# Empty bytes between pools and tiles of a four-layer trunk: other distances between the streamed and the held row of a matmul

## The chip, the cores and the metric

The kernel runs on one core of a Trainium2 chip. The metric is the device time of one launch in microseconds (us). The core has five engines that work side by side, each through its own instruction queue: TensorE (PE) multiplies matrices, VectorE (DVE) and ScalarE (ACT) work element by element, GpSimd (POOL) does small work and starts some transfers, and SyncE (SP) starts most transfers. PE reads two operands from the on-chip memory (SBUF): one that it holds (the weights of the array, loaded ahead; "PEld" in the profile) and one that it streams through, row by row of each partition. Tiles lie in SBUF at byte addresses that the tile pools give out one after another, alike in all 128 partitions.

## The reference

A sequence of 512 vectors of 1,024 numbers in fp32 passes four layers. Each adds a mixer and a SwiGLU feed-forward block (FFN) to the sequence:

```python
for layer in range(4):
    h = rmsnorm(x, norm_mix[layer])
    mix = s5(h) | gla(h) | diff_attention(h) | s5(h)       # layers 0, 1, 2, 3
    x = x + mix
    h = rmsnorm(x, norm_ffn[layer])
    g, u = split(h @ w_gate_up[layer])                      # 1024 -> 2 x 2816
    x = x + (silu(g) * u) @ w_down[layer]                   # 2816 -> 1024
return rmsnorm(x, norm_final)
```

S5 is a complex diagonal recurrence with an output projection (1024 to 2048), GLA is gated linear attention with four heads, the third mixer is differential attention with eight pairs of heads.

## The kernel before, in words

**Arithmetic.** Each fp32 operand of a large product is split into a high part (a rounded copy, `fp32r`) and a low part (what the rounding left), and a product is three matmuls: high by high, high by low, low by high (`mm3`, lines 351 to 353). A weight block is brought by a DMA of 512 KB into a staging tile `wst` (L324, three buffers), cast by ACT into the first half of a tile `whl` (L334, "high", five buffers) and completed by DVE (L338, "low").

**Which row is streamed.** Three forms carry nearly all of PE's time. In `gemm_b` (L351 to L353, `acc<-whl,X`) PE streams 512 columns of the weights `whl` and holds 128 columns of the activations X: `hT` (normed input, transposed), `act` (FFN hidden), `zT` (S5 output), `oT` (output of the attention mixers). In `gemm_a` (`any<-hT,whl`) it streams 512 columns of `hT` and holds the weights. In `seven_product` (L566, the gate and up product of the FFNs of layers 1 to 3, seven products where the plain way needs eight) it streams 256 columns of a tile `sides` or `side` and holds the weights. `sides` are the parts named "11" and "12"; they lie in a buffer of the `hT` pool. The parts "1", "2", "3", "4", "22" are tiles `side...` in the FFN's own pool. A product over one block of 256 hidden columns is 24 matmuls in a row.

**Pools.** `const`, `xp`, `hp` (`hT`), `wp` (`wst`, `whl`), `normp` and `small` stay for the whole program, in this order. Each mixer and each FFN opens a pool of its own behind them, and the next stage's pool lies over the same addresses. A tile laid over one of an earlier stage waits for that tile's last reader; the pool library works this out. The `zT` pools lie at the other end of the memory.

**What sets the order around the change.** Instructions are mostly in an order worked out by a scheduler; at the ends of mixers and the starts of FFNs `hand_all()` fixes the order as written. Before an FFN of layers 1 to 3 starts its first two blocks a and b, SP issues in a row (L599, L324): `slot0`, the first `lent`, `slot1`, the second `lent`, `slot2`, two `wst`, `gain`, one `wst`. `slot0` and `slot1` hold part "21" of the weights; `lent` holds part "1", onto which POOL adds a second block by an accumulating DMA (L602). The order written out there begins: `split21a one:a split21b square flush one:b total1 ... two:a two:b split1b ... five:a ...`. "split21a" is the cast and the low part of `slot0`; "one" and "two" stream `sides` (`a<-sides`, `d<-sides`), "two" with the weights of the slots; "five" streams `side1` with the weights of `lent` (`c<-side`).

In `normed` (L446 to L461) ACT squares a row block and sums it into a tile `ms`, DVE adds eps (L437), POOL raises to -1/2 (L439, `rs`), and the block is scaled.

Of the kernel before, what the change touches and what calls it, by code (L numbers as in the profile page):

```python
# [11 lines left out]
F32 = mybir.dt.float32  # L12
# [9 lines left out]
P = 128  # L22
D = 1024
SEQ = 512
NT = SEQ // P
# [35 lines left out]
class Left:  # L61
# [15 lines left out]
    def room(self):  # L77
        self.hT = [self.tr.hp.tile([P, KT, SEQ], F32R, tag="hT", name=f"hT{z}") for z in range(2)]
# [184 lines left out]
class Trunk:  # L263
    def __init__(self, ctx, tc, ins, out):
        self.ctx, self.tc, self.nc = ctx, tc, tc.nc
        self.i = ins
        self.out = out
        self.rot = 0
        nc = self.nc
        ep = lambda name, bufs, **k: ctx.enter_context(tc.tile_pool(name=name, bufs=bufs, **k))  # L270
        self.cp = ep("const", 1)
        self.xp = ep("xp", 1)
        self.hp = ep("hp", 2)
        self.wp = ep("wp", 3)
        self.np_ = ep("normp", 2)
        self.sp = ep("small", 8)
        self.ps = ep("psum", 1, space=PSUM)
        self.dp = ep("dram", 1, space=DRAM)
        self.ident = self.cp.tile([P, P], F32, name="ident")
        make_identity(nc, self.ident)  # L280
        self.two_pi = float(np.nextafter(np.float32(TWO_PI), np.float32(0)))
        self.mhalf = self.cp.tile([P, 8], F32, name="mhalf")
        nc.vector.memset(self.mhalf[:], -0.5)
        self.ones = self.cp.tile([P, P], F32, name="ones")
        nc.gpsimd.memset(self.ones[:], 1.0)
        self.dq = nc.sync
        self.jobs = iter(())
        self.pend = []
        self.guard, self.lazy = None, False

    def hand_all(self):
        E = mybir.EngineType
# [149 lines left out]
    def normed(self, xt, g, out, pool, aside=False):  # L442

        nc = self.nc
        if pool is None:
            junk = self.wp.tile([P, D], F32, tag="wst", name="sq", bufs=3)  # L446
        else:
            junk = pool.tile([P, D], F32, tag="sq", name="sq", bufs=2)
        ms = self.sp.tile([P, 1], F32, tag="ms", name="ms")
        nc.scalar.activation(junk[:], xt, AF.Square, scale=1.0 / 32.0, accum_out=ms[:])  # L450
        r = self.rsqrt(ms[:], 1, 1e-6)
        if out is None:
            h = pool.tile([P, D], F32, tag="h", name="h", bufs=2)
            nc.vector.scalar_tensor_tensor(h[:], xt, r[:], g[:], op0=ALU.mult, op1=ALU.mult)
            return h
        if aside:
            nc.scalar.mul(junk[:], xt, r[:])
            gr = lambda y: y.rearrange("p (g c) -> p g c", c=16)
            nc.gpsimd.tensor_tensor(out, gr(junk[:]), gr(g[:]), op=ALU.mult)
            return  # L460
        nc.vector.scalar_tensor_tensor(  # L461
            out, xt.rearrange("p (g c) -> p g c", c=16), r[:],
            g[:].rearrange("p (g c) -> p g c", c=16), op0=ALU.mult, op1=ALU.mult,
        )
# [40 lines left out]
    def ffn_plain(self, l, left, after=None, aside=None):  # L505

        nc, i = self.nc, self.i
        wgu, wd = i["ffn_w_gate_up"][l], i["ffn_w_down"][l]
        nxt = None
        with self.tc.tile_pool(name=f"ffn{l}", bufs=1, reuse_waits="tile") as fp:  # L510
            self.jobs = aside(fp) if aside else iter(())
            first = True
            j0 = 0
            for nh in (12, 10):
                acts = []
                for jp in range(j0, j0 + nh, 2):
                    hls, banks = [], []
                    for j in (jp, jp + 1):
                        for half in range(2):
                            hls.append(self.wa(wgu, half * FFN_HIDDEN + j * P))  # L520
                            banks.append(self.anybank())
                            if not first:
                                self.gemm_a(left.hT, hls[-1], banks[-1])
                        if not first:
                            acts.append(self.glu(fp, left.R, banks[-2], banks[-1]))
                            next(self.jobs, None)
                    if first:
                        self.gemm_a4(left, hls, banks)
                        for m in range(2):
                            acts.append(self.glu(fp, left.R, banks[2 * m], banks[2 * m + 1]))  # L530
                        first = False
                        next(self.jobs, None)
                stat = lambda k, part, t: acts[k][:, part, t * P : (t + 1) * P]
                if j0 and after is not None:
                    nxt = Left(self, after)
                for d in range(2):
                    tail = 4 if (d == 1 and j0) else 0
                    self.gemm_b(stat, wd, nh, d * 512, self.add_x(d, nxt, left.r), k0=j0, tail=tail)
                j0 += nh
            for _ in self.jobs:  # L540
                pass
        return nxt
# [169 lines left out]
    def ffn(self, l, left, after=None, turn=False, aside=None):  # L712
# [5 lines left out]
        with self.tc.tile_pool(name=f"ffn{l}", bufs=1, reuse_waits="tile") as fp:  # L718

            room = lambda: fp.tile([P, 2, 4, 256], F32, tag="act", name="lent", bufs=4)  # L720
            left.open(fp, ("1", "2", "4", "3", "22") if l < 3 else ("1", "2"))
            if l == 3:
                lent = room()
            slots = [fp.tile([P, 4, 256], F32, name=f"slot{n}") for n in range(SLOTS)]

            if l < 3:
                lent = room()
            self.jobs = aside(fp) if aside else iter(())
            blocks = [self.seven_block(fp, slots, left, wgu, b, turn) for b in range(FFN_HIDDEN // 256)]
            f = blocks[:2]  # L730
# [15 lines left out]
            for step in plan.split():  # L746
                name, _, n = step.partition(":")
# [633 lines left out]
    def s5_first(self, ctx):  # L1381
        nc, i = self.nc, self.i
        xin = self.xp.tile([P, NT, D], F32, tag="x", name="xin")
        zpool = ctx.enter_context(self.tc.tile_pool(name="zT0", bufs=1, side="right"))
        zT = zpool.tile([P, 2, KT, SEQ], F32R, name="zT")
        with self.tc.tile_pool(name="s5_0", bufs=1) as p:
            scr, more = (self.hp.tile([P, 4096], F32, tag="hT", name=f"scr{z}") for z in range(2))
            oms = [more[:, 1024 * z : 1024 * z + 1024].rearrange("p (a b) -> p a b", a=2) for z in range(2)]
# [73 lines left out]
    def s5_second(self, l, ctx, left):  # L1462
        nc = self.nc
        zpool = ctx.enter_context(self.tc.tile_pool(name="zT1", bufs=1, side="right"))
        zT = zpool.tile([P, 2, KT, SEQ], F32R, name="zT")
        with self.tc.tile_pool(name="s5_1", bufs=1) as p:
            room = p.tile([P, 6, 512], F32, name="room2")
            parts = (("in", 0, 2, 2), ("cs", 2, 5, 3), ("out", 5, 8, 2))
            ops = {}

            def get(kk, name):
                if name == "r4":
                    return ops[kk, "cs"][:, 2]
                if name == "map":
                    return ops[kk, "out"][:, 2]
                return ops[kk, name]

            def loads(kk, names):
                for name, a, b, bufs in parts:
                    if name in names:  # L1480
                        o = p.tile([P, b - a, 512], F32, tag=name, name=name, bufs=bufs)
                        nc.sync.dma_start(o[:], self.spill[kk][:, a:b])
                        ops[kk, name] = o

            def steps(kk):
                if kk + 1 < 8:
                    loads(kk + 1, ("in", "cs"))
                if 1 <= kk < 9:
                    loads(kk - 1, ("out",))

            loads(0, ("in", "cs"))
            accs = self.s5_pipe(1, left.hu, zT, False, room, get, steps, left)
        return self.s5_glu(1, zT, accs, self.i["norm_ffn"][l])
# [32 lines left out]
    def gla(self, l, left, after):  # L1526
# [3 lines left out]
        wo = i["gla_w_o"][0]  # L1530
        self.hand(mybir.EngineType.PE)
        with self.tc.tile_pool(name="gla", bufs=1) as p:
            big = lambda name, tag="g8", bufs=5: p.tile([P, 4, 512], F32, tag=tag, name=name, bufs=bufs)
            late = lambda name: big(name, "g8late", 3)
            oT = [p.tile([P, 2, 4, SEQ], F32R, name="oT0"), None]
# [108 lines left out]
            def readout(hf, t):  # L1644
                st, o_h = sts[hf], on[hf]
                oo = row(self.tp("op"))
                ms = self.sp.tile([P, 2], F32, tag="ms2", name="ms")
                for z in range(2):
                    h = 2 * hf + z
                    zs = slice(z * 256, (z + 1) * 256)  # L1650
# [139 lines left out]
    def diff(self, l, left, after):  # L1790
# [2 lines left out]
        w, wo = i["diff_w_qkv"][0], i["diff_w_o"][0]  # L1793
        self.hand(mybir.EngineType.PE)
        with self.tc.tile_pool(name="diff", bufs=1) as p:
            T = lambda tag, bufs=2: p.tile([P, 512], F32, tag=tag, name=tag, bufs=bufs)
            oT = [p.tile([P, 2, 4, SEQ], F32R, name="oT0"), None]
            qks = [p.tile([P, 2, 4, SEQ], F32, tag="qk", name="qk", bufs=2) for _ in range(2)]
# [157 lines left out]

            def normalised(j):
                st, o_s = kept.pop(j)
                q2 = self.sp.tile([P, NT], F32, tag="q2", name="q2")
                v.tensor_tensor(q2[:], st[:, 0], st[:, 0], op=ALU.mult)  # L1960
                v.scalar_tensor_tensor(q2[:], q2[:], 1e-5, st[:, 1], op0=ALU.mult, op1=ALU.add)
                rs = self.rsqrt(q2[:], NT, 0.0)
# [50 lines left out]
            for i in range(32):  # L2013
# [5 lines left out]
                if i in (15, 28, 31):  # L2019
                    n = (0, 0)  # L2020
# [117 lines left out]
```

## Time and profile before

| | us |
|---|---|
| median of 3 runs | 2384.86 (2382.88 to 2385.13) |
| the profiled execution's own time | 2382.31 |
| its span in the profile | 2380.6 |
| PE busy | 2269.0 (95%) |
| DVE busy | 1487.1 (62%) |
| ACT busy | 1073.0 (45%) |
| POOL busy | 266.8 (11%) |

The mean TensorE clock granted over the span is 0.982 of full speed. PE's busy time is not to be read as work at full rate: a matmul's record lasts until its modelled end, and the next one starts while it still runs. What a matmul costs the path is the distance from one start to the next, and that is read from stretches in which PE waits for nothing: from the chain of work, which merges consecutive matmuls of one line and gives their time and count, or from a window of fixed length and the count of matmuls in it.

### The profile page before, as it was taken

The page shows a single profiled execution, that of the slowest core. Times are in us where ns is not written, and L with a number is a line of the kernel's source. Part 1 is how long each engine was busy: PE and PEld are TensorE (multiplying, and loading weights), DVE is VectorE, ACT ScalarE, POOL GpSimd, SP SyncE. Part 2 cuts the span into 40 slices and gives each one's busy share as a digit, 9 for nine tenths or more (in the row PEclk, how much of TensorE's full clock was granted, in tenths as well). Part 3 has the DMA queues.
Part 4 walks back from the last instruction along what each step waited for, and adds up shares of the span by engine and source line. Part 5 has one row for each costly group of instructions (what it writes and reads, how often), then busy time and mean ns, then how long its engine had stood idle before and what let it go on. Part 6 is the DMA issues. An engine that isn't in the chain of part 4 may idle for free. (4 is left out here: it accounts for less than half of the span.)

```text
span 2380.6 us, 35208 instructions
## 1 busy us (share of the span) xinstructions
PE 2269.0 (95%) x14055; PEld 1962.8 (82%) x14055; DVE 1487.1 (62%) x2311; ACT 1073.0 (45%) x1749; POOL 266.8 (11%) x335
## 2 busy tenths in 40 slices
PE   4799999999999999999999998989999899999997
PEld 3578888788877789898987887888989788999996
DVE  7774565555443459585753666875847874967674
ACT  4463445444352346252544665653635233634442
POOL 3330100111000011010001221110000000101000
PEclk9699999999999999999999999999999899999999
DMA  4123344544332258564345465694732645666521
GB/s 110 34 52 138 95 138 143 166 129 166 118 103 85 71 143 208 137 177 124 111 142 117 107 133 145 170 243 115 195 98 89 214 158 150 170 179 154 162 76 67
DMA packets 275502, 317.42 MB, mean 133 GB/s; under 512 B 45653, under 2 KB 214377, under 8 KB 274058
## 3 DMA queue, kind: packets, MB, share of 16 engines
q1 hardware_dynamic: 227210, 238.14, 31.9%
q0 software_dynamic: 48128, 77.02, 15.7%
q8 instruction: 111, 1.82, 0.3%
q14 instruction: 53, 0.43, 0.1%
HBM read 275.92 MB, written 23.99 MB: 126 GB/s over the span
## 5 line engine op out<-in xcount | busy, mean ns | idle before, releaser
L338 DVE TENSOR_TENSOR whl<-wst,whl 128x1024 fp32r<-128x1024 f32 x294 | 359.0, 1223 | 363.1 <-ACT whl L334 362.3
L334 ACT CAST whl<-wst 128x1024 fp32r<-128x1024 f32 x294 | 308.4, 1050 | 530.5 <-PE acc L353 354.8
L566 PE MATMUL a<-side,whl 128*128 128x256 f32 x2376 | 291.2, 279 | 14.2 <-ACT r L638 6.0
L566 PEld LDWEIGHTS a<-side,whl 128*128 128x128 f32 x2376 | 281.4, 190 | 16.2 <-ACT whl L334 6.9
L351 PE MATMUL acc<-whl,act 128*128 128x512 f32 x704 | 276.5, 393 | 0.7 <-DVE g L611 0.7
L353 PE MATMUL acc<-whl,act 128*128 128x512 f32 x704 | 276.9, 393 | 0.0
L352 PE MATMUL acc<-whl,act 128*128 128x512 f32 x704 | 275.6, 391 | 0.0
L566 PE MATMUL c<-side,whl 128*128 128x256 f32 x1584 | 192.4, 278 | 3.6 <-DVE whl L338 3.6
L566 PEld LDWEIGHTS c<-side,whl 128*128 128x128 f32 x1584 | 186.9, 189 | 4.0 <-DVE whl L338 4.0
L351 PEld LDWEIGHTS acc<-whl,act 128*128 128x128 f32 x704 | 132.2, 188 | 30.9 <-DVE g L611 1.9
L352 PEld LDWEIGHTS acc<-whl,act 128*128 128x128 f32 x704 | 132.2, 188 | 28.8
L353 PEld LDWEIGHTS acc<-whl,act 128*128 128x128 f32 x704 | 132.3, 188 | 27.9
L351 PE MATMUL any<-hT,whl 128*128 128x512 f32 x384 | 151.7, 395 | 0.0
L352 PE MATMUL any<-hT,whl 128*128 128x512 f32 x384 | 149.6, 390 | 0.0
L353 PE MATMUL any<-hT,whl 128*128 128x512 f32 x384 | 149.6, 389 | 0.0
L351 PE MATMUL acc<-whl,hT 128*128 128x512 f32 x352 | 143.8, 408 | 1.1 <-ACT whl L334 0.6
L352 PE MATMUL acc<-whl,hT 128*128 128x512 f32 x352 | 138.6, 394 | 1.0 <-DVE whl L338 1.0
L353 PE MATMUL acc<-whl,hT 128*128 128x512 f32 x352 | 139.0, 395 | 0.0
L338 DVE TENSOR_TENSOR whl<-halves,whl 128x1024 fp32r<-128x1024 f32 x72 | 87.7, 1222 | 32.5 <-ACT whl L334 32.5
L352 PE MATMUL acc<-whl,zT 128*128 128x512 f32 x256 | 103.9, 406 | 4.1 <-DVE whl L338 4.1
L334 ACT CAST whl<-halves 128x1024 fp32r<-128x1024 f32 x72 | 75.3, 1052 | 69.2 <-PE acc L353 26.7
L351 PE MATMUL acc<-whl,zT 128*128 128x512 f32 x256 | 102.8, 406 | 2.7 <-ACT zT L468 2.7
(438 smaller groups left out, 4185.1 us busy)
## 6 DMA issues: line engine op xcount, KB each, us to landing
wst<-in_ffn_w_gate_up_dram SPq DMA_DIRECT2D x110, 512.0 KB, 4.0
wst<-in_ffn_w_down_dram SPq DMA_DIRECT2D x88, 512.0 KB, 3.7
halves<-in_ffn_w_gate_up_dram SPq DMA_DIRECT2D x42, 512.0 KB, 5.9
slot<-in_ffn_w_gate_up_dram SPq DMA_DIRECT2D x39, 512.0 KB, 6.6
wst<-in_ffn_w_gate_up_dram POOLq DMA_DIRECT2D x33, 512.0 KB, 6.4
wst<-in_s_w_glu_dram SPq DMA_DIRECT2D x32, 512.0 KB, 3.6
spill<-opsp POOLq DMA_DIRECT2D x8, 2048.0 KB, 8.7
wst<-in_gla_w_in_dram SPq DMA_DIRECT2D x24, 512.0 KB, 3.6
```

Source lines behind the costliest of these rows:

```text
L334: self.nc.scalar.copy(hl[:, 0], w[:])
L338: self.nc.vector.tensor_tensor(hl[:, 1], w[:], hl[:, 0].bitcast(F32), op=ALU.subtract)
L351: mm(out, lh, rh, start=first, stop=False)
L352: mm(out, lh, rl, start=False, stop=False)
L353: mm(out, ll, rh, start=False, stop=last)
L566: mm(o, hl[:, x, k, c], side[:, y, k], start=first and not (j or k or n), stop=k == 3 and n == 2, skip_group_check=True,)
```

## The change

A helper `edge(pool, n)` puts an empty tile of n bytes per partition into a pool. It is called in eight places; nothing reads or writes these tiles, and all they do is move the tiles behind them. To make room, three small tiles of the `small` pool get fewer buffers than the pool's eight (`ms` 2, `ms2` 4, `q2` 2).

```diff
+    def edge(self, pool, n):
+        if n:
+            pool.tile([P, n // 4], F32, name=f"edge{n}", bufs=1)
...
         self.wp = ep("wp", 3)
+        self.edge(self.wp, 64)
...
-        ms = self.sp.tile([P, 1], F32, tag="ms", name="ms")
+        ms = self.sp.tile([P, 1], F32, tag="ms", name="ms", bufs=2)
...
         with self.tc.tile_pool(name=f"ffn{l}", bufs=1, reuse_waits="tile") as fp:
+            self.edge(fp, 160)
             self.jobs = aside(fp) if aside else iter(())
...
             if l == 3:
+                self.edge(fp, 320)
                 lent = room()
+                self.edge(fp, 192)
             slots = [fp.tile([P, 4, 256], F32, name=f"slot{n}") for n in range(SLOTS)]
             if l < 3:
+                self.edge(fp, 128 * l)
                 lent = room()
...
         zT = zpool.tile([P, 2, KT, SEQ], F32R, name="zT")
+        self.edge(zpool, 416)
...
         zT = zpool.tile([P, 2, KT, SEQ], F32R, name="zT")
+        self.edge(zpool, 352)
...
         with self.tc.tile_pool(name="gla", bufs=1) as p:
+            self.edge(p, 128)
...
-                ms = self.sp.tile([P, 2], F32, tag="ms2", name="ms")
+                ms = self.sp.tile([P, 2], F32, tag="ms2", name="ms", bufs=4)
...
         with self.tc.tile_pool(name="diff", bufs=1) as p:
+            self.edge(p, 192)
...
-                q2 = self.sp.tile([P, NT], F32, tag="q2", name="q2")
+                q2 = self.sp.tile([P, NT], F32, tag="q2", name="q2", bufs=2)
```

**Distances.** The addresses that the built programs give the tiles yield, for each form of matmul, the distance from the held row's first byte to the streamed row's first byte. Within a form it is the same for all its matmuls if it is taken modulo 256 bytes, so it is given that way (columns are how many columns are streamed):

| matmuls | columns | count | before | after |
|---|---|---|---|---|
| `a<-side`, `c<-side` | 256 | 3960 | 192 | 192 |
| `a<-sides`, `d<-sides` | 256 | 1584 | 0 | 192 |
| `any<-hT,whl` (FFN of layer 0) | 512 | 1152 | 0 | 192 |
| `acc<-whl,hT` (GLA and attention input) | 512 | 1056 | 0 | 64 |
| `acc<-whl,act` (layers 0, 1, 2, 3) | 512 | 4 x 528 | 64 | 160, 192, 64, 0 |
| `acc<-whl,zT` (first, second S5) | 512 | 2 x 384 | 224 | 192, 128 |
| `acc<-whl,oT` (GLA, attention) | 512 | 2 x 192 | 64 | 192, 128 |
| `s<-ks,qs` (scores) | 512 | 128 | 64 | 128 |

For `side` the streamed row itself moves from 128 to 192 past a multiple of 256, and the held one from 192 to 0; for `sides` the streamed row stays at 192 and the held one moves from 192 to 0.

**Order.** PE's and POOL's instructions stand in the same order as before; what else moves is in the first part of S5 in layer 0. One wait is new. At the border between GLA and the FFN of layer 1, SP's row of loads stands so before (the brackets name the semaphores that an instruction waits for, by the engine that raises them):

```order
235 L324 DMA wst<-in_ffn_w_gate_up_dram 128x4x256 [waits DMAHW7_49,DVE_49]
236 L599 DMA slot_6737<-in_ffn_w_gate_up_dram 128x4x256 [waits PE_49,Pool_49]
237 L599 DMA lent<-in_ffn_w_gate_up_dram 128x4x256 [waits PE_49]
238 L599 DMA slot_6738<-in_ffn_w_gate_up_dram 128x4x256
239 L599 DMA lent<-in_ffn_w_gate_up_dram 128x4x256
240 L599 DMA slot_6739<-in_ffn_w_gate_up_dram 128x4x256
```

And in the changed kernel, where the lines of the code are 6 or 7 further down:

```order
235 L330 DMA wst<-in_ffn_w_gate_up_dram 128x4x256 [waits DMAHW7_49,DVE_49]
236 L606 DMA slot_6741<-in_ffn_w_gate_up_dram 128x4x256 [waits DVE_49,PE_49,Pool_49]
237 L606 DMA lent<-in_ffn_w_gate_up_dram 128x4x256
238 L606 DMA slot_6742<-in_ffn_w_gate_up_dram 128x4x256
239 L606 DMA lent<-in_ffn_w_gate_up_dram 128x4x256
240 L606 DMA slot_6743<-in_ffn_w_gate_up_dram 128x4x256
```

The first slot now waits for DVE too, and the first `lent` for nothing of its own. The values waited for changed with it. `slot0` of that FFN now begins 448 bytes lower (173504 instead of 173952), and GLA's last tile, which holds the second half of `oT`, now ends 128 bytes inside it (at 173632; before it ended at 173952, where the slot began). So the PE semaphore's value that `slot0` waits for is that of the last matmul `acc<-whl,oT` of GLA, where before it was that of a matmul of GLA's gates about 155 us earlier, and the four loads behind `slot0` in SP's queue come after it.

In the head of the program (S5 of layer 0) DVE's row, before, around the scaling of the input (`scr<-xin,rs,gain`):

```order
112 L1033 TENSOR_TENSOR X<-X,dx 128x8x48
113 L437 TENSOR_SCALAR ms<-ms 128x1 x2
114 L1032 TENSOR_TENSOR dx<-X,pw 128x384
115 L1031 TENSOR_TENSOR X<-bb,s5fr 128x8x16
116 L1033 TENSOR_TENSOR X<-X,dx 128x8x48
117 L461 SCALAR_TENSOR_TENSOR scr_95<-xin,rs,gain 128x64x16 x2
```

And in the changed kernel:

```order
112 L1043 TENSOR_TENSOR X<-X,dx 128x8x48
113 L443 TENSOR_SCALAR ms<-ms 128x1
114 L1041 TENSOR_TENSOR X<-bb,s5fr 128x8x16
115 L1042 TENSOR_TENSOR dx<-X,pw 128x384
116 L1041 TENSOR_TENSOR X<-bb,s5fr 128x8x16
117 L1043 TENSOR_TENSOR X<-X,dx 128x8x48
118 L467 SCALAR_TENSOR_TENSOR scr_97<-xin,rs,gain 128x64x16
119 L443 TENSOR_SCALAR ms<-ms 128x1
120 L1042 TENSOR_TENSOR dx<-bb,s5fi 128x128
121 L467 SCALAR_TENSOR_TENSOR scr_97<-xin,rs,gain 128x64x16
```

The last `ms` (of four row blocks; there are two buffers now) comes behind the first scaling, and the second scaling behind it. On ACT the fourth Square moves from ahead of `CAST params` to between the two casts of `frow`, and on SP four `bpad` and two `bb` loads go ahead of the three `wst` loads.

## The prediction

> **What bounds the kernel.** I read the page's head first, then the chain, then stretches in which PE waits for nothing.
>
> ```profile
> span 2380.6 us, 35208 instructions
> PE 2269.0 (95%) x14055; PEld 1962.8 (82%) x14055; DVE 1487.1 (62%) x2311; ACT 1073.0 (45%) x1749; POOL 266.8 (11%) x335
> PE 33%; DVE 5%; ACT 2%; DMA 1%; issue 1%; POOL 0%; ACTq 0%; DVEq 0%; POOLq 0%
> ```
>
> PE is busy 95% of the span, next comes DVE at 62%, so what a matmul costs from start to start is nearly the whole time. The change touches that cost, and I need it for each form. In the chain, four neighbours of the seven products in FFN 2 (start, time, engine, name, line, count):
>
> ```profile
> 1653.08 2.86 PE d L566 x24
> 1655.94 2.74 PE a L566 x24
> 1658.68 2.72 PE c L566 x24
> 1669.72 2.72 PE a L566 x24
> ```
>
> The first streams `sides` (distance 0), the others `side` (distance 192; the 2.74 behind a `sides` group takes part of its end along). Same code, same 24 matmuls of 256 columns: 2.86 us against 2.72, so 119.2 ns a matmul against 113.3. For 512 columns I take windows within one form (busy, count, clock, DMA); a window of T holds as many records as start in T plus one record's 0.39 us, so the start-to-start time is (T + 0.39) / count.
>
> ```profile
> 316.00:336.00 20.00, 20.00 (x90) 1.00 0.41 119
> 1250.00:1268.00 18.00, 18.00 (x81) 1.00 0.00 1
> 1084.00:1126.00 42.00, 42.00 (x186) 1.00 0.40 100
> 860.00:869.00 9.00, 9.00 (x41) 1.00 0.80 131
> 1986.00:2018.00 32.00, 32.00 (x139) 1.00 0.85 217
> ```
>
> They are `any<-hT` (distance 0): 20.39 / 90 = 226.6 ns; `acc<-hT` (0): 227.0; `acc<-act` (64): 227.9, and a count of 185 would make it 229.1, so 228.5; `acc<-oT` (64): 229.0; `acc<-zT` (224): 233.0, and by 138 234.7, so 233.8. The clock is full in all, and the DMA share does not order them. So time goes with distance, by up to 7 ns of 227, but I have rows only for 0, 64 and 224 at 512 columns, and for 0 and 192 at 256.
>
> **The change, part by part.** *`sides`, 0 to 192.* 1584 matmuls are 66 groups of 24; each should take what `side` takes at 192: 66 x (2.72 - 2.86) = -9.2 us. `side` stays at 192: nothing.
>
> *`acc<-hT`, 0 to 64.* 1056 x (228.8 - 226.9 = 1.9 ns) = +2.0 us, both ends from rows.
>
> *`act`.* Layer 3, 64 to 0: 528 x -1.8 = -1.0 us. Layer 2 stays. Layer 0, at 160, has no near row: between 226.6 and 233.8 it is -1.0 to +2.8; I take 0, its own price. Layer 1, at 192, see next.
>
> *512 columns at 192* (`any`, `act` of layer 1, `zT` of the first S5, `oT` of GLA: 1152 + 528 + 384 + 192 = 2256 matmuls). No row. One end is the row nearest in distance, 224: 233.8 ns. The other is the row of the same distance at 256 columns, which saves 6 ns against 0: 226.7 - 6 = 220.7 ns. The two rows are as near as each other, so I take their middle, 227, the time at distance 0. Then `any` 0, `act` 528 x -1.5 = -0.8, `zT` 384 x -6.8 = -2.6, `oT` 192 x -2 = -0.4: -3.8 us. Each ns of that price is 2.26 us.
>
> *512 columns at 128* (`zT` of the second S5, `oT` of the attention, the scores: 384 + 192 + 128). Nearest is 64, 228.5 ns: 384 x -5.3 = -2.0 us, else 0; bounds 0 and -2.7.
>
> *Distances in sum:* -9.2 + 2.0 - 1.0 - 3.8 - 2.0 = -14.0 us.
>
> *The new wait (GLA to FFN 1).* What SP issued there before, POOL's first sum behind it, and how long such loads took to land (issue to landing, in that stretch):
>
> ```profile
> 841.16 0.46 SPq L599 DMA_DIRECT2D slot<-in_ffn_w_gate_up_dram  x1
> 841.67 0.50 SPq L599 DMA_DIRECT2D lent<-in_ffn_w_gate_up_dram  x1
> 843.62 1.21 SPq L599 DMA_DIRECT2D slot<-in_ffn_w_gate_up_dram  x1
> 849.61 1.38 POOL L602 DMA_DIRECT2D lent<-in_ffn_w_gate_up_dram  x1 [40.39 <-DVE x L496]
> slot<-in_ffn_w_gate_up_dram SPq DMA_DIRECT2D x3, 512.0 KB, 8.3
> lent<-in_ffn_w_gate_up_dram POOLq DMA_DIRECT2D x2, 512.0 KB, 7.5
> ```
>
> And what used them:
>
> ```profile
> 876.01 0.40 PE L353 MATMUL acc<-whl,oT 128*128 128x512 f32 x1
> 876.60 3.12 PE L566 MATMUL a<-sides,whl 128*128 128x256 f32 x24
> 877.36 2.00 ACT L334 CAST whl<-slot 128x1024 fp32r<-128x1024 f32 x2
> 878.45 2.36 DVE L338 TENSOR_TENSOR whl<-slot,whl 128x1024 fp32r<-128x1024 f32 x2 [0.53 <-ACT whl L334]
> 882.86 5.92 PE L566 MATMUL d<-sides,whl 128*128 128x256 f32 x48
> 883.03 1.05 ACT L334 CAST whl<-lent 128x1024 fp32r<-128x1024 f32 x1
> 885.56 1.22 DVE L338 TENSOR_TENSOR whl<-lent,whl 128x1024 fp32r<-128x1024 f32 x1
> 888.62 5.62 PE L566 MATMUL c<-side,whl 128*128 128x256 f32 x48
> ```
>
> SP's row now starts when the last `oT` matmul has ended, at 876.4 instead of 841.2. If it repeats what it did then, `lent` with its sum is complete 849.61 + 7.5 - 841.16 = 16.0 us later, at 892.4; its cast and low part take 1.05 + 1.22 more, and product "five", whose third matmul needs the low part, starts in full at 894.7 instead of 888.6: +6.1 us. The first slot lands 8.3 us on, at 884.7; behind ACT's cast of it wait the copies of the transposes and the other casts, behind DVE's low part the sums for "five" (back to back from 878.45 to 888.6), which so come up to 7 us later and agree. Against it: at 841 two `wst` loads of 512 KB were still on their way, which at 876 are not, so it may land sooner; +3 us is the lower end (half of that), 9 the upper (five's operands 7 us late by both engines, and a later load 2 us more). Then PE has stood still for some us, and elsewhere in the program that costs clock:
>
> ```profile
> 1575.61 2.90 PE L566 MATMUL c<-side,whl 128*128 128x256 f32 x24
> 1584.54 5.02 PE L566 MATMUL a<-side,whl 128*128 128x256 f32 x24 [6.04 <-ACT r L638]
> 1584.00:1588.00 4.00, 3.46 (x16) 0.50 0.49 160
> ```
>
> After 6 us of idle PE the granted clock was 0.50 and the 24 matmuls took 5.02 us instead of 2.9: 2.1 us more. So the wait costs 6 + 2 = 8 us, 3 to 11. The Trainium skill (TensorE: Matmul & The Clock Gate, "What's actually happening") names a window of about 3.4 us without work as what halves the clock; the row agrees, and by that rule the 2 us stay away if the idle time splits into parts shorter than that.
>
> *The head.* The second scaling `scr` now comes behind the last `ms`, which itself comes behind the first scaling:
>
> ```profile
> 28.59 0.20 DVE L437 TENSOR_SCALAR ms<-ms 128x1 f32<-128x1 f32 x2
> 32.64 1.08 POOL L439 TENSOR_TENSOR rs<-ms,mhalf 128x1 f32<-128x1 f32 x2
> 33.23 2.48 DVE L461 SCALAR_TENSOR_TENSOR scr<-xin,rs,gain 128x1024 f32<-128x1024 f32 x2 [3.31 <-POOL rs L439]
> 35.82 1.51 ACT L1167 COPY room<-xps 64x256 f32<-64x256 f32 x4 [4.62 <-DVE scr L461]
> 36.62 0.28 PEld L1001 LDWEIGHTS rough<-counts,frow 12*128 12x128 f32 x1 [4.07 <-ACT room L1167]
> 60.52 1.05 ACT L334 CAST whl<-wst 128x1024 fp32r<-128x1024 f32 x1
> ```
>
> Two scalings take 2.48, so the first ends at 34.47; `ms` (0.1, two in 0.20), its power on POOL (0.54) and the steps between engines (some 0.25 by the gap from 32.64 + 0.54 to 33.23 and its like) put the second at about 35.4 instead of 34.47. ACT's `room` and PE's `rough` wait for it in turn: +0.9 us on the path (0 to 1.5, if `frow`'s cast behind the moved Square is felt too). The `wst` loads, which SP issued by 33 and now issues behind the `bpad` and `bb` ones, are first cast at 60.5 (the last row): nothing, unless they come 20 us later. At the end of the program:
>
> ```profile
> 2370.49 1.04 ACT L450 ACTIVATE sq<-x 128x1024 f32<-128x1024 f32 x1
> 2370.82 0.55 POOL L439 TENSOR_TENSOR rs<-ms,mhalf 128x1 f32<-128x1 f32 x1 [1.47 <-DVE ms L437]
> 2372.60 0.21 DVE L437 TENSOR_SCALAR ms<-ms 128x1 f32<-128x1 f32 x2
> ```
>
> The fourth Square now waits until that power has read its buffer, 2371.37, and ends 0.9 later, with its sum at 2372.6, when DVE's scaling before lets it come to the `ms` anyway: 0.1. The other small buffers (`ms2`, `q2`) cost nothing I can find, since their last readers are steps of an earlier block.
>
> *Sum:* -14.0 + 8 + 1.0 = -5.0 us. The profiled execution took 2382.31 (its span of 2380.6 and 1.7 around it), which makes 2377.3; it lies 2.55 below the median of the runs, 2384.86, and against that the forecast is 2379.9.
>
> **Rivals.** *1. At 192, 512 columns behave as at 224* (slower). Then the 2256 matmuls cost 233.8: +6.8 x 2.26 = +15.3 on the sum, so +10.3, 2395. It decides from a price of 227 + (5.0 + 4.8) / 2.26 = 231.3 ns on. For it: 224 is only 32 bytes off, and the four 512-column rows know no distance below 226.6. Against it: at 256 columns 192 is the better one.
>
> *2. At 192, 512 columns save as 256 do* (much faster): 220.7 ns, -14.0 on the sum, so -19, 2366. For it: `any` and `sides` share tile, pool and distance 0. Against it: no row shows 512 columns below 226.6.
>
> *3. Distance does nothing,* and the rows differ by something else that goes with the form. Then only the wait and the head are left: +9.0, 2393.9. The Trainium skill (SBUF — State Buffer, "SBUF: two separate sides" and "Who interferes with whom") gives PE two independent read ports, one for the streamed and one for the held operand, neither of which waits for anyone; by that rule addresses can't matter. This case's 119.2 against 113.3 ns speaks against it: `d` and `c` differ in no count, engine or clock, only in where their tiles lie.
>
> *4. It is the streamed row's own place, not the distance.* In `sides` it lies at 64 modulo 128 and is slow, in `side` at 0 and is fast; now both lie at 64. The 3960 `side` matmuls would go from 113.3 to 119.2: +23.4, and `sides` would keep its 2.86; 2380 + 9 + 23 = 2412. Against it: `any`, `act` and `zT` stream from the same place modulo 256 (192) and differ by 7 ns.
>
> *5. The wait costs the upper end or more* (12 us: POOL's second sum queues behind the first): -1, 2384, no change. Or it is covered (3 us): -10, 2375.
>
> **How the numbers follow.** A change of 0.2%, 4.8 us, is about what a measurement of this kernel can tell. The forecast 0.36 (its size is uncertain by some 5 us from the prices at 160 and 192 and from the wait: faster 0.20, same 0.14, slower 0.02). Rival 1 0.15 (slower); rival 2 0.20 (faster); rival 3 0.09 (slower); rival 4 0.05 (slower); rival 5, dear 0.11 (same 0.08, slower 0.03), covered 0.04 (faster). In sum faster 0.44, same 0.22, slower 0.34. The range from 2363 to 2396 reaches to rivals 1, 2 and 3 and leaves out rival 4 and the far ends of rival 2 and of the wait, under 2 in 10; the likeliest case alone spans 2374 to 2386.
>
> **What would show it.** `sides` groups of 24 at 2.72 us in the chain (at 2.86: rival 3; `side` at 2.86: rival 4). A window of `any` in FFN 0 of 20 us with 90 records (87 or 88: rival 1; 92 or 93: rival 2). `acc<-hT` at 80 in 18 us, `zT` at 141 or more in 32 us. SP's first `slot` load of FFN 1 at about 876 of the old time, PE idle ahead of "two" or "five" for 4 to 8 us, and a granted clock of 0.5 behind. The page's chain with another engine than PE in FFN 0 or in the seven products would make the whole working wrong, since a gain per matmul would then not reach the end.

## The result and the profile after

The changed kernel takes 2408.29 us (median of 4 runs, 2404.68 to 2410.21), the one before 2384.99 beside it: slower by 0.9%, ratio 1.009 with a 95% interval of 1.0066 to 1.0115. The forecast was 2379.9 and the range 2363 to 2396, so both the sign and the range were wrong. The profiled execution took 2410.21 us, 27.9 more than that of before. The page's head and its chain by engine:

```profile
span 2408.5 us, 35210 instructions
PE 2289.9 (95%) x14055; PEld 1969.5 (82%) x14055; DVE 1486.6 (62%) x2311; ACT 1071.5 (44%) x1749; POOL 267.8 (11%) x335
PE 32%; DVE 7%; ACT 2%; DMA 1%; issue 1%; POOL 0%; ACTq 0%; DVEq 0%; POOLq 0%
```

PE is busy 20.9 us longer with the same 14055 matmuls, the other engines as long as before: the time went into the matmuls themselves, and a part into waits (DVE's share of the chain, 5% to 7%). The windows that answer to those of before, in the same runs of matmuls:

```profile
321.00:341.00 20.00, 20.00 (x87) 1.00 0.40 115
1277.00:1295.00 18.00, 18.00 (x80) 1.00 0.01 2
1109.00:1151.00 42.00, 42.00 (x181) 1.00 0.40 100
2012.00:2044.00 32.00, 32.00 (x139) 1.00 0.83 215
```

`any`, now at 192, fits 87 times into 20 us, where 90 did: 234.4 ns by (T + 0.39) / count against 226.6 (a count that is one off moves this by 2.7 ns; the table below goes matmul by matmul). `acc<-hT`, at 64, takes 229.9 against 227.0; `act` of layer 1, at 192, 234.2 against 227.9 to 229.1; `zT`, from 224 to 128, 233.0 as before. The clock is full in all of them.

The products of 256 columns, from the chain, in two blocks of FFN 2 (start, time, engine, name, line, count):

```profile
1676.69 2.72 PE a L573 x24
1679.41 2.72 PE d L573 x24
...
1797.56 2.83 PE a L573 x24
1800.39 2.83 PE d L573 x24
```

`d` streams `sides`, the `a` ahead of it `side`; all are at 192 now. In one block every group takes 2.72 us, 113.3 ns a matmul, in another every group 2.83, 117.8 ns. The distances are the same in both, and the granted clock is 1.00 in both (1676 to 1684 and 1797 to 1806); what differs is the stretch of the program. In the chain's lines for groups of 24, 56 stand at 2.83 and 23 at 2.72 or 2.73. Before, where nothing waited, only `sides` took 2.86 or more, and `side` was at 2.72 to 2.74 but for six lines at 2.83. These six are three pairs, each behind the first `sides` group that follows a piece of 512 columns; the next `sides` group ends the slow rate. One of the pairs, in the chain of before:

```profile
2157.26 2.83 PE c L566 x24
2160.09 2.83 PE a L566 x24
2162.91 2.87 PE d L566 x24
2165.79 2.74 PE a L566 x24
```

At the border of GLA and FFN 1, from the timeline (start, length, engine):

```profile
890.24 0.40 PE L359 MATMUL acc<-whl,oT 128*128 128x512 f32 x1
890.71 0.37 SPq L606 DMA_DIRECT2D slot<-in_ffn_w_gate_up_dram  x1
894.90 1.05 ACT L340 CAST whl<-slot 128x1024 fp32r<-128x1024 f32 x1 [3.19 <-DMA slot<-in_ffn_w_gate_up_dram]
896.91 1.38 POOL L609 DMA_DIRECT2D lent<-in_ffn_w_gate_up_dram  x1 [74.20 <-DMA lent<-in_ffn_w_gate_up_dram]
901.00 2.86 PE L573 MATMUL d<-sides,whl 128*128 128x256 f32 x22 [0.72 <-DVE whl L344]
906.83 1.04 ACT L340 CAST whl<-lent 128x1024 fp32r<-128x1024 f32 x1 [3.67 <-DMA lent<-in_ffn_w_gate_up_dram]
907.93 0.50 PE L573 MATMUL c<-side,whl 128*128 128x256 f32 x2 [4.07 <-ACT whl L340]
909.19 3.10 PE L573 MATMUL c<-side,whl 128*128 128x256 f32 x13 [0.76 <-DVE whl L344]
```

and the window behind it:

```profile
908.00:912.00 4.00, 3.24 (x15) 0.59 1.19 243
```

SP's first slot load stands behind GLA's last matmul, product "five" (`c`) waits 4.07 us for the cast of `lent`, and the clock drops to 0.59 behind it. That part came as forecast.

Where the 27.9 us went, by setting each matmul's start in one trace beside the same matmul's in the other (steady: both start-to-start times undisturbed):

| part | matmuls | ns each, before to after | us |
|---|---|---|---|
| `any`, 0 to 192 | 1152 | 227.3 to 233.3 | +6.8 |
| `act`, 64 to 160, 192, 64, 0 | 2112 | 229.0 to 234.2, 233.3, 229.0, 226.8 | +3.6 |
| `hT` to 64, `oT` to 192 and 128, `zT` | 2208 | 228.1 to 229.4; 229.5 to 232.9; 233.1 as before | +2.3 |
| `sides`, 0 to 192 | 1584 | 119.4 to 115.6 | -5.9 |
| `side`, 192 as before | 3960 | 113.9 to 115.5 | +6.2 |
| GLA to FFN 1, 876 to 925 of the old time | | | +9.6 |
| head, 0 to 60, 60 to 130, 130 to 155 | | | +0.3, -1.5, +4.6 |
| the rest | | | +1.9 |

### The profile page after: what moved, and what is told of

The parts are those of the page before. It is cut to its first block, busy times and chain, and to the rows that moved or that the text cites. A ratio compares the mean times of both kernels' runs of the same rounds, so it can differ in the third digit from the quotient of the medians.

```text
span 2408.5 us, 35210 instructions
## 1 busy us (share of the span) xinstructions
PE 2289.9 (95%) x14055; PEld 1969.5 (82%) x14055; DVE 1486.6 (62%) x2311; ACT 1071.5 (44%) x1749; POOL 267.8 (11%) x335
## 5 line engine op out<-in xcount | busy, mean ns | idle before, releaser
L573 PE MATMUL a<-side,whl 128*128 128x256 f32 x2376 | 299.3, 283 | 15.7 <-ACT whl L340 6.4
L573 PEld LDWEIGHTS a<-side,whl 128*128 128x128 f32 x2376 | 288.5, 193 | 18.3 <-ACT whl L340 7.4
L357 PE MATMUL any<-hT,whl 128*128 128x512 f32 x384 | 153.8, 400 | 0.0
L358 PE MATMUL any<-hT,whl 128*128 128x512 f32 x384 | 151.8, 395 | 0.0
L359 PE MATMUL any<-hT,whl 128*128 128x512 f32 x384 | 151.8, 395 | 0.0
```

Source lines behind the costliest of these rows:

```text
L357: mm(out, lh, rh, start=first, stop=False)
L358: mm(out, lh, rl, start=False, stop=False)
L359: mm(out, ll, rh, start=False, stop=last)
L573: mm(o, hl[:, x, k, c], side[:, y, k], start=first and not (j or k or n), stop=k == 3 and n == 2, skip_group_check=True,)
```

## The experiments

Before was run again beside each of two sets: 2387.08 us (median of 17 runs) for experiments 1 to 4, 2386.15 (15 runs) for 5 to 8.

**1. Distance by itself.** A kernel that streams from one tile and holds from another:

```diff
+def seg(name, n, d, count, shift=0, stall=False):
...
+    for k in range(count):
+        s0 = (k % 15) * P + shift // 4
+        m0 = (k % nb) * n + (d + shift) // 4
...
+        nc.tensor.matmul(bank[:, :n], S[:, s0 : s0 + P], M[:, m0 : m0 + n], start=k == 0, stop=k == count - 1)
```

> A kernel of its own: it computes nothing of the reference, only runs of fp32r matmuls from one held tile and one streamed tile, 48 of 256 columns or 36 of 512, at 16 distances (0 to 240 bytes by 16), entered from a stall, from 512 columns at distance 0, and from 256 columns at distance 0; at the end distances 0 and 192 with both rows moved by 64, 128 and 192 bytes. Theory (distance decides, and at 256 columns a run can lock into one of two rates): 512 columns at 0, 64, 128, 160, 192, 224 take 226.7, 229.0, 232.8, 234.2, 233.3, 233.1 ns start to start; 256 columns at 0 take 119.4; at 192 they take 113.3 behind a run at distance 0 and 113.3 or 117.8 behind a stall or behind 512 columns; moving both rows alike changes nothing. Rival (the streamed row's own place decides): the last part differs with the place by 4 ns or more at 256 columns. Rival (something else of the kernel decides): all distances alike within 1 ns.

Its timeline; a row's length is 47 start-to-start times and one last record of 0.28 us at 256 columns, 35 and one of 0.39 at 512. The names say what ran ahead, the columns and the distance:

```profile
78.34 5.76 PE L40 MATMUL stall256at112x<-streamed,held 128*128 128x256 f32 x48 [0.36 <-ACT sums L41]
109.68 5.72 PE L40 MATMUL stall256at192x<-streamed,held 128*128 128x256 f32 x48 [0.36 <-ACT sums L41]
136.90 5.92 PE L40 MATMUL after512at000x<-streamed,held 128*128 128x256 f32 x48
196.08 5.64 PE L40 MATMUL after512at112x<-streamed,held 128*128 128x256 f32 x48
238.03 5.82 PE L40 MATMUL after512at192x<-streamed,held 128*128 128x256 f32 x48
331.89 5.66 PE L40 MATMUL after256at112x<-streamed,held 128*128 128x256 f32 x48
374.51 5.62 PE L40 MATMUL after256at192x<-streamed,held 128*128 128x256 f32 x48
551.45 8.35 PE L40 MATMUL wide512at000x<-streamed,held 128*128 128x512 f32 x36
663.73 8.58 PE L40 MATMUL wide512at160x<-streamed,held 128*128 128x512 f32 x36
686.21 8.57 PE L40 MATMUL wide512at192x<-streamed,held 128*128 128x512 f32 x36
757.30 5.82 PE L40 MATMUL place256at192by064x<-streamed,held 128*128 128x256 f32 x48
765.83 5.62 PE L40 MATMUL place256at192by128x<-streamed,held 128*128 128x256 f32 x48
782.48 8.37 PE L40 MATMUL place512at000by064x<-streamed,held 128*128 128x512 f32 x36
826.95 8.57 PE L40 MATMUL place512at192by128x<-streamed,held 128*128 128x512 f32 x36
```

At 256 columns distance 0 gives (5.92 - 0.28) / 47 = 120.0 ns. Distance 192 gives 113.3 behind a run at 0 or a stall (their first three starts are slower), but 117.8 behind 512 columns, and it stays there for all 48. Distance 112 comes to 113.3 from all three. At 512 columns 0 gives 226.7 once steady, 160 234.3, 192 233.3; of the 16 distances only 0 is below 228. The run-up counts there too: 64 gives 228.9 behind a stall and 233.3 behind 256 columns, where 229.0 was expected for both. Where both rows are moved by 64 or 128 bytes, 512 columns don't change once steady. At 256 columns and 192 one of the three places came out at 117.8 and two at 113.3, which are the two rates that this distance has anyway. The slow one has the rows where `side` and its weights lay in the kernel before (128 and 192 past a multiple of 256), which ran at 113.3 there, so the place is not its cause; but a run at 0 stood ahead of it, so that alone does not promise the fast rate in every case. Distance decides, not the row's own place, and at 192 the run-up decides with it, in a way that these rows give only in part.

**2. The wait taken away from the changed kernel.**

```diff
+            self.edge(fp, 256 * (l == 1))
             left.open(fp, ("1", "2", "4", "3", "22") if l < 3 else ("1", "2"))
```

> The changed kernel with 256 more bytes ahead of the pool of FFN 1, so that slot0 no longer lies over the end of GLA's oT; every distance modulo 256 stays. Theory (the overlap's wait costs 9.3 us where GLA meets FFN 1): 9 us less than the changed kernel, about 2399 beside 2385 of before, SP's first slot load at about 854 instead of 890. Rival (the time was lost to clock and phases of PE, which differ by run): within 3 us of the changed kernel, 2405 to 2411.

2397.40 us (12 runs): 10.9 less than the changed kernel (13.0 if each is set against before run beside it), 1.005 of before (1.0034 to 1.0067). One of the runs, at 4538.75 us, is not explained; without it the median is 2397.08. SP's loads are early again:

```profile
851.70 0.46 SPq L606 DMA_DIRECT2D slot<-in_ffn_w_gate_up_dram  x1
```

Against before, the stretch from 876 to 925 now differs by -0.5 us instead of +9.6. `side` is slower by 7.8 us in this run, since about six in ten of its groups are at 2.83, where in the changed kernel's own trace it is half.

**3. Distance 0 given back to `any`, `hT` and `sides`.**

```diff
-        self.edge(self.wp, 64)
+        self.edge(self.hp, 64)
```

> The changed kernel with the 64 bytes ahead of the hT pool instead of in the weights' pool: any, sides and hT are back at distance 0, all else stays, the places of side and of the weights too. The new wait stays. Theory (two rates at 192, and each run of sides at 0 puts side back into the fast one): side mean from 115.5 to 113.9 ns (-6.3 us), sides 115.6 to 119.4 (+6.0), any 233.3 to 227.3 (-7.0), hT 229.4 to 228.1 (-1.3): 8.6 us less than the changed kernel, about 2400. Rival (side is slower for the place of its rows, 192 and 0 past 256, not for what runs before it): side stays at 115.5, and the kernel gains 2.3 us only, about 2406.

2399.66 us (6 runs): 8.6 less than the changed kernel, where 8.6 was forecast. That the two agree to the tenth is chance: the runs lie up to 4.8 us apart (2398.72 to 2403.54), and set against before run beside each the gain is 10.7. The places of `side` and of the weights are those of the changed kernel, but the chain reads again:

```profile
1708.87 2.74 PE c L573 x24
1711.61 2.72 PE a L573 x24
1714.33 2.86 PE d L573 x24
1717.19 2.74 PE a L573 x24
```

No group of the chain stands at 2.83 any more; matmul by matmul `side` is within 0.3 ns of before, `sides` and `any` within 0.1. Of the forms in these blocks only `sides` changed its distance, so it is the runs of `sides` at distance 0, at 2.86 us, that put the following `side` groups back into the fast rate. Not every one does: the pairs at 2.83 in the chain of before stand behind a first one, and the second one of the block ends them. Moving `sides` to 192 took that away.

**4. All matmuls of 512 columns at distance 0.** Before, with other empty bytes (an excerpt: the FFN of layer 0, the pool of FFN 1, ahead of `lent`, both S5, GLA and attention; `ms2` has 6 and `q2` 2 buffers to make room):

```diff
+            self.edge(fp, 64)
...
+            self.edge(fp, 256 * (l == 1))
...
+                self.edge(fp, 64)
                 lent = room()
...
+        self.edge(zpool, 32)
...
+            self.edge(p, 64)
```

> The kernel before with other empty bytes: every matmul of 512 columns at distance 0 (any and hT are there already; act, zT, oT and the scores are moved), sides at 0 and side at 192 as before, no new overlap, order as before (of the small tiles only ms2 and q2 get fewer buffers). Theory (distance decides, 0 is best at 512 columns): act 2112 x -2.25 ns, zT 768 x -6.4, oT 384 x -2.7, scores 128 x -5: -11.3 us against before, about 2374, faster by 0.47%. Rival (distance is not the cause): same as before within 3 us.

2379.14 us (6 runs), 0.9962 of before (0.9946 to 0.9977): 9 us by the ratio, where 11.3 were expected. Windows of `zT` in the second S5 and of `act` in layer 1:

```profile
1982.00:2009.00 27.00, 27.00 (x120) 1.00 0.90 240
1080.00:1115.00 35.00, 35.00 (x156) 1.00 0.49 121
```

27.39 / 120 = 228.3 ns against 233.0 to 234.7, and 35.39 / 156 = 226.9 against 227.9 to 229.1. In the traces `act` saves 3.9 us, `zT` 3.7 and `oT` 0.3, the scores nothing, where 0.6 was expected of them. `zT` and `oT` fall short of their price (768 x 6.4, 384 x 2.7): many of their runs are short, and the first four starts of a run take some 231 to 232 ns even at distance 0, the later ones 227 to 228.

**5. The wait by itself,** in the kernel before:

```diff
         with self.tc.tile_pool(name="gla", bufs=1) as p:
+            p.tile([P, 64], F32, name="edge256", bufs=1)
```

> The kernel before with one thing of the change: 256 empty bytes ahead of GLA's tiles, so that the end of oT lies under slot0 of FFN 1; every distance modulo 256 stays. Theory (the overlap's wait costs 9 to 10 us by itself): 9.6 us more than before, nearly all of it between 876 and 925 of the old time, with SP's first slot load behind GLA's last matmul. Rival (the loss there needed the slow rate or the clock of the changed kernel): under 5 us more.

2395.20 us (4 runs), 1.0042 of before (1.0027 to 1.0057), 9 to 10 us. In the trace the stretch from 876 to 925 takes 9.6 us more:

```profile
876.11 0.37 SPq L599 DMA_DIRECT2D slot<-in_ffn_w_gate_up_dram  x1
893.59 0.80 PE L566 MATMUL c<-side,whl 128*128 128x256 f32 x2 [4.55 <-ACT whl L334]
```

The same price in the old distances as in the new: the wait has nothing to do with the rates. And `oT` of GLA, moved here by 256 bytes against the weights, keeps its rate within 0.2 ns, as it should if the distance counts modulo 256.

**6. The small buffers by themselves.**

```diff
-        ms = self.sp.tile([P, 1], F32, tag="ms", name="ms")
+        ms = self.sp.tile([P, 1], F32, tag="ms", name="ms", bufs=2)
...
+                ms = self.sp.tile([P, 2], F32, tag="ms2", name="ms", bufs=4)
...
+                q2 = self.sp.tile([P, NT], F32, tag="q2", name="q2", bufs=2)
```

> The kernel before with one thing of the change: fewer buffers for ms (2), ms2 (4) and q2 (2), which brings the other order at the head and moves all stages' pools by 512 bytes, so no distance changes. Theory: 0.3 to 1 us more in the first 60 us, and nothing behind: same as before. Rival (the 4.6 us that the changed kernel lost between 130 and 155 come from that order): 4.6 us more there as well.

2386.41 us (10 runs), ratio 1.000 (0.9983 to 1.0016): nothing that can be measured. The trace has +0.2 us up to 60, -2.0 to 130 and +3.2 from 130 to 155, so part of the changed kernel's 4.6 us there. Windows of 10 us there, of before, of the changed kernel, of this one, and of experiment 2, which has the changed kernel's instructions in this stretch:

```profile
140.00:150.00 10.00, 9.75 (x72) 1.00 0.10 20
```
```profile
140.00:150.00 10.00, 10.00 (x35) 0.53 0.03 7
```
```profile
140.00:150.00 10.00, 10.00 (x47) 0.66 0.01 2
```
```profile
140.00:150.00 10.00, 9.53 (x71) 1.00 0.09 17
```

With the same instructions the clock is 0.53 in one trace (the second) and 1.00 in another (the last), so no instruction there sets it by itself. Which one a run gets, and whether the new order makes the slow one more frequent, stays open: of the traces with the new order four of five show a loss of 3 us or more there, of the three with the old order none (one lost 1.4), and the medians of this experiment say that it is not worth 0.2%.

**7. 256 columns at 112,** the distance that the first experiment found, on top of experiment 4 (an excerpt):

```diff
-        two = self.tr.hp.tile([P, 2, 2, 4, 256], F32R, tag="hT", name="sides")
+        two = self.tr.hp.tile([P, 4096 + 64], F32R, tag="hT", name="sides")
+        two = two[:, 28 : 28 + 4096].rearrange("p (s z a n) -> p s z a n", s=2, z=2, a=4)
...
+        five = pool.tile([P, 2048 * len(names) + 4], F32R, name="side" + names[0])
+        for j, n in enumerate(names):
+            self.place[n] = five[:, 4 + 2048 * j : 2052 + 2048 * j].rearrange("p (z a n) -> p z a n", z=2, a=4)
```

> The kernel with all 512-column matmuls at distance 0, and now side and sides at 112 (their slices begin 16 or 112 bytes inside larger tiles; nm, st, sums, ms, ms2 and q2 with fewer buffers to make room; no overlap with oT). Theory (at 112 a run of 256 columns falls into 113.3 ns from wherever it comes): sides 119.4 to 113.4 (1584 x -6.0 = -9.5 us), side 113.9 to 113.4 (3960 x -0.5 = -2.0), on top of the -8 us that distance 0 at 512 columns has shown: 19 us less than before, about 2366, faster by 0.8%. Rival (the sweep's rates don't carry over, with weights changing from block to block): no faster than the kernel with 0 at 512 columns, 2379.

2368.30 us (5 runs, 2365.64 to 2370.08), 0.9927 of before (0.9915 to 0.9939), 17 to 18 us: faster than both kernels. The chain has hardly a group that is not at 2.72:

```profile
1668.02 2.72 PE d L574 x24
1670.74 2.72 PE a L574 x24
1673.46 2.72 PE c L574 x24
```

`sides` saves 9.1 us and `side` 1.8, against 9.5 and 2.0 expected. This trace, too, lost 4.6 us between 130 and 155.

**8. Distances by 4 bytes,** the first experiment's kernel with `for d in range(0, 256, 4)`:

> A kernel of its own, as the first sweep (nothing of the reference is computed): distances 0 to 252 bytes by 4, 48 matmuls of 256 columns behind 512 columns at 0, then 36 of 512 columns behind 256 at 0. [...]

The question was whether a distance between the multiples of 16 is faster than the best of them.

```profile
275.47 5.64 PE L40 MATMUL after512at112x<-streamed,held 128*128 128x256 f32 x48
283.69 6.04 PE L40 MATMUL after512at116x<-streamed,held 128*128 128x256 f32 x48
581.38 8.35 PE L40 MATMUL wide512at000x<-streamed,held 128*128 128x512 f32 x36
773.02 8.80 PE L40 MATMUL wide512at068x<-streamed,held 128*128 128x512 f32 x36
```

No distance beats 0 at 512 columns (226.7 ns once steady; 68 is among the worst, 240.0) or 112 at 256 (113.3 once steady; four bytes on, at 116, 122.4). The next best at 256 behind 512 columns are 32 and 144, at 116.7.

## Why the prediction was wrong, point by point

- **That distance decides: right.** Rivals 3 (no effect) and 4 (the streamed row's own place) fell with experiments 1 and 3; and in the change itself the streamed rows of `any` and `sides` stayed where they were and the times moved. The rule of the Trainium skill that was set against it (SBUF — State Buffer, "SBUF: two separate sides": PE's two read ports wait for no one) does not describe what these runs show, 226.7 to 240.0 ns for the same matmul by distance alone. What in the chip makes the distance cost time, no run here shows.
- **512 columns at 192: the step that failed first.** The prediction had two ends as near as each other, 233.8 (the row at 224) and 220.7 (the saving that 256 columns have at 192), and took their middle, 227. It measured 233.3: rival 1, with its row. On 2256 matmuls that is some 14 us. Alone it would have ended at rival 1's 2395, inside the range; the next two points, 9.5 us together, and smaller ones led beyond it. Carrying a saving from 256 columns to 512 was the mistake: in the sweep 256 columns take 120.0 ns at 0 and least at 112 and 192, while 512 columns take least at 0.
- **`side` stays at 192, "nothing": the step that failed next.** It became 6.2 us slower in this trace and 7.8 in experiment 2. A steady rate was read as a property of the distance; it belonged to the distance and to what ran ahead. The chain of before had the sign of it in its three pairs of `side` groups at 2.83 us: the second rate was there, and a `sides` group ended it each time. What sets the rate of a stretch in the changed kernel, beyond that nothing at distance 0 puts it back, stays open.
- **`sides`: right in direction, 5.9 instead of 9.2 us,** for the same reason: at 192 it is at 117.8 about half of the time.
- **`act` at 160 and 128 for `zT`:** 160 was taken at its own price and cost 5.2 ns each, +2.7 us; `zT` at 128 was to save 2.0 us and saved nothing (232.8), at 192 was to save 2.6 and saved nothing.
- **The new wait: right.** 8 us forecast, 3 to 11 as its range, 9.6 measured, twice; the first slot landed 4.2 us after its issue rather than 8.3, so "two" was late by less than 1 us, but `lent` and its sum took the time: issue at 890.71 to cast at 906.83 is 16.1 us, where the prediction had 16.0. The third matmul of "five" starts 20.3 us later than before, 14.2 of which were lost ahead of the border: 6.1 for the wait, as forecast. The other 3.5, forecast as 2, came mostly with the low clock and one more wait of 0.8 us behind it.
- **The head: right at its steps, and soon gone.** `rough` starts 0.7 us later (37.33 instead of 36.62), where 0.9 was forecast; at 60 us 0.3 of it is left, and between 60 and 130 us 1.5 are gained. But 4.6 us came between 130 and 155 with a lower clock, which no term held; experiment 6 leaves its cause open.

With what was measured in their places, the sum reads: distances +13.0 (6.8 + 3.6 + 2.3 - 5.9 + 6.2) instead of -14.0, the wait 9.6 instead of 8, the head -1.2 instead of 1.0, or +3.4 where the clock is low at 140: 21 to 26 us, around the 23.3 of the medians.

## What to carry to other kernels

Where PE streams fp32r rows back to back, each matmul with a weight load of its own (nothing else was measured here), the distance of the streamed from the held row, modulo 256 bytes, is a parameter like a tile size: measure it for each width in a small kernel by itself, from more than one run-up, before placing tiles. A rate that is read in one place may be kept alive by its neighbour: ask what runs ahead of it, and whether the change moves that as well. And bytes put between pools are no neutral thing: check which earlier tile each later one now lies over, since 128 bytes of overlap cost as much here as the best placement of a whole form saved.

## What was not expected of the hardware

- At one distance (192 bytes, 256 columns) a run of matmuls has two steady rates, 113.3 and 117.8 ns, and where nothing breaks in it keeps the one it fell into, in the changed kernel for up to 28 groups of 24 in a row, from one piece of 512 columns to the next.
- The rates are fine in the address: at 256 columns 112 bytes give 113.3 ns, 108 bytes 119.5 and 116 bytes 122.4; at 512 columns 0 bytes 226.7 and 4 bytes 237.5.
